# Layer 0's modulation in quarters of the features, with five products of the first layer opened between them

## The chip, the cores and the metric

The kernel runs on one core of a Trainium2 chip. The metric is the device time of one execution in microseconds (us). Engines are named as in the profile: PE is TensorE's matmuls, PEld its weight loads, DVE is VectorE, ACT is ScalarE, POOL is GpSimd, SP is SyncE, whose queue issues all DMAs here.

## What is computed

A trunk of two layers over 256 context tokens and 256 tokens of the sequence (1024 features), then a stack of attention, a recurrent mixer and two feed-forward blocks. What the change touches is the beginning of a trunk layer:

```python
silu_c, silu_cc = silu(c), silu(c_ctx)
mod   = silu_c  @ mod_w[l] + mod_b[l]        # 1024 -> 3072, for the sequence
mod_c = silu_cc @ mod_w[l] + mod_b[l]        # the same weights, for the context
shift, scale, gate = split(mod, 3)
z  = (rmsnorm(x,  pre_g) * (1 + scale)   + shift)   @ w_in     # 1024 -> columns q, kv, kr, ..., merge
zc = (rmsnorm(xc, pre_g) * (1 + scale_c) + shift_c) @ w_in
```

The columns of `w_in` are read in blocks of 128: `q` 0 and 1, `kv` 0 and `misc` (rope and gate columns) are the latents of the first attention, `px` and `pg` belong to the pool branch, `merge` to the merging gates. Everything is float32.

## The kernel before, in words

*Products.* Each weight block of up to 128 x 1024 numbers (512 KB) is loaded into a tile `wr` (`raw`, L361) and split into a high part `wh` (ScalarE, L377) and a low part `wl` (VectorE, L379). Activations are split in the same way (`split`, L385 and L386). A product of one block with all 512 tokens is 8 blocks of the contraction times three matmuls of 512 columns, high by high, low by high and high by low (`mm3`, L395 to L397), 24 matmuls that add up in one PSUM buffer. Of PSUM's eight buffers three are `mm`, three `at`, two `aux`.

*The head.* The four token tiles are loaded, normed (L429, L1175) and transposed into `xT`, features by tokens (L1179, L1180). Meanwhile the modulation runs in `mod_cols`: 2048 columns of `mod_w` in four stages of 512 columns in the order shift 0 to 511, scale 0 to 511, shift 512 to 1023, scale 512 to 1023. A stage has four loads of 512 KB; each load is multiplied with both silu vectors in small matmuls (L466), and behind the fourth `mod_rows` copies the sums out (L470), `mod_cols` transposes them (L479), adds up four groups (L482), adds the bias (L483) and for a scale stage applies 1 + scale and the norm's gain (L486). After the second stage the features 0 to 511 of `xT` are scaled and shifted (L1188) and split into `xn`, after the fourth the other half. The sixteen loads have sixteen buffers of their own.

*Layer 0.* Only then come the weight blocks of the layer: `latents` makes q0, q1, kv and misc, each with its evacuations, and column sums for the norms (L669, L671), reciprocal roots, transposes (L445) and tables. `weaves` runs a main generator and takes steps of filling generators at a given ratio per step: beside the latents and the attention (`mla`) these are the pool branch (8 steps: px0, pg0, px1, ...) and the first merge (8 steps), beside the attention also the second layer's modulation, beside the scan (`gla`) the rest of the merge, four gate steps and eight merge steps. A level of the scan is subtractions on VectorE, an exponential, two multiplications on GpSimd (L895, L915) and small matmuls (L859).

*Order.* The framework puts the instructions of each engine and queue into an order ahead of time, from the program's order, the readiness that its own time table gives, the free buffers and priorities; `high_priority` moves work ahead, and `tc.issue_after(i)` puts the instructions of a block behind instruction `i` on `i`'s engine. On the chip each engine takes its instructions in that order.

## Time and profile before

| | |
|---|---|
| median of three runs | 1546.4 us (1542.88 to 1547.67) |
| profiled execution | 1548.55 us, its span 1546.7 us |
| TensorE busy | 1485.1 us, 96% of the span |
| VectorE / ScalarE / GpSimd busy | 62% / 49% / 16% |
| read from HBM | 227.09 MB, 147 GB/s over the span |

The profile is one execution. Matmuls are pipelined and their ends are modelled, so the durations of neighbouring matmuls overlap; what one costs in a dense stretch is the distance between starts. Idle time of an engine that is not the bottleneck costs nothing.

### The profile page before, as it was taken

What the parts mean: (1) busy time and instruction counts of PE and PEld (TensorE: products, weight loads), DVE (VectorE), ACT (ScalarE), POOL (GpSimd) and SP (SyncE); (2) the same over time, 40 slices, a digit from 0 to 9 for tenths busy, and PEclk for the clock granted to TensorE, in tenths of its full rate; (3) what the DMA queues carried; (4) which work ended last, traced back from release to release, by engine and by line L of the source; (5) the groups of instructions that cost most, each with busy time, mean ns of one, the idle gap of its engine ahead of it and who ended that gap; (6) DMA issues with size and microseconds to landing.
All of it is one profiled execution on the core that took longest, in us unless ns stands there. A gap on an engine that the chain in (4) does not pass through costs nothing.

```text
span 1546.7 us, 25517 instructions
## 1 busy us (share of the span) xinstructions
PE 1485.1 (96%) x10206; PEld 1277.8 (83%) x10206; DVE 955.3 (62%) x1530; ACT 757.8 (49%) x1267; POOL 248.5 (16%) x225
## 2 busy tenths in 40 slices
PE   6999999999999999999999989999999997899998
PEld 3766668787877789878989989879999886899986
DVE  5555545866444567766786654866665567756654
ACT  4444344463423356656565454554444458534443
POOL 0101103624200000113442020321000024100000
PEclk8999999999999999999999999999999998899999
DMA  8433322223334465326446563324566654435564
GB/s 341 126 101 131 123 91 82 65 68 95 96 109 151 135 207 160 116 76 207 158 149 193 170 224 124 123 95 157 185 187 185 214 191 148 151 116 186 180 191 134
DMA packets 65639, 229.79 MB, mean 149 GB/s; under 512 B 7280, under 2 KB 7920, under 8 KB 65392
## 3 DMA queue, kind: packets, MB, share of 16 engines
q1 hardware_dynamic: 65520, 228.16, 46.0%
q8 instruction: 80, 1.31, 0.3%
q14 instruction: 39, 0.32, 0.1%
HBM read 227.09 MB, written 1.05 MB: 147 GB/s over the span
## 4 chain that ended last, share of the span: by engine, by line
PE 81%; DVE 6%; DMA 4%; issue 3%; ACT 3%; POOL 2%; SPq 0%; POOLq 0%; DVEq 0%; ACTq 0%
PE mm L395 22%; PE mm L397 22%; PE mm L396 22%; DMA wr<-in_w_dram 3%; PE at L735 2%; DVE wl L379 2%; PE aux L768 2%; ACT wh L377 2%; PE at L755 1%; PE at L859 1%; PE mm L466 1%; POOL wl L379 1%; POOL E L915 1%; POOL qp L895 1%; PE aux L466 0%
## 5 line engine op out<-in xcount | busy, mean ns | idle before, releaser
L379 DVE TENSOR_TENSOR wl<-wr,wh 128x1024 fp32r<-128x1024 f32 x339 | 425.5, 1257 | 340.2 <-ACT wh L377 338.5
L377 ACT ACTIVATE wh<-wr 128x1024 fp32r<-128x1024 f32 x352 | 370.6, 1055 | 426.3 <-PE mm L396 149.7
L395 PE MATMUL mm<-xnah,wh 128*128 128x256 f32 (+1 forms) x1192 | 368.9, 310 | 11.5 <-DVE rt L1496 10.3
L397 PE MATMUL mm<-xnah,wl 128*128 128x256 f32 (+1 forms) x1192 | 363.2, 305 | 4.0 <-DVE wl L379 4.0
L396 PE MATMUL mm<-xnal,wh 128*128 128x256 f32 (+1 forms) x1192 | 361.7, 304 | 0.0
L395 PEld LDWEIGHTS mm<-xnah,wh 128*128 128x128 f32 x1192 | 226.9, 190 | 27.4 <-DVE rt L1496 10.5
L397 PEld LDWEIGHTS mm<-xnah,wl 128*128 128x128 f32 x1192 | 226.8, 190 | 17.3 <-DVE wl L379 5.4
L396 PEld LDWEIGHTS mm<-xnal,wh 128*128 128x128 f32 x1192 | 227.1, 191 | 9.7 <-issue 1.4
L419 POOL TENSOR_TENSOR sm<-sm,minus_half 128x1 f32<-128x1 f32 (+3 forms) x34 | 26.3, 776 | 695.3 <-DVE sm L567 357.6
L397 PE MATMUL mm<-xnbh,wl 128*128 128x512 f32 (+1 forms) x392 | 136.7, 349 | 0.0
L395 PE MATMUL mm<-xnbh,wh 128*128 128x512 f32 (+1 forms) x392 | 135.0, 345 | 0.0
L396 PE MATMUL mm<-xnbl,wh 128*128 128x512 f32 (+1 forms) x392 | 134.8, 344 | 0.0
L395 PE MATMUL mm<-wh,xnah 128*128 128x256 f32 x288 | 83.4, 291 | 6.4 <-ACT xnah L385 6.1
L397 PEld LDWEIGHTS mm<-xnbh,wl 128*128 128x128 f32 x392 | 73.9, 188 | 11.8 <-issue 3.1
L395 PEld LDWEIGHTS mm<-xnbh,wh 128*128 128x128 f32 x392 | 74.0, 189 | 11.2 <-issue 2.9
L397 PE MATMUL mm<-wh,xnal 128*128 128x256 f32 x288 | 82.2, 289 | 0.8 <-DVE xnal L386 0.6
L396 PE MATMUL mm<-wl,xnah 128*128 128x256 f32 x288 | 82.7, 289 | 0.0
L396 PEld LDWEIGHTS mm<-xnbl,wh 128*128 128x128 f32 x392 | 73.9, 188 | 10.1 <-issue 1.2
L396 PE MATMUL mm<-wl,hh 128*128 128x512 f32 x176 | 69.1, 393 | 0.2 <-DVE wl L379 0.2
L397 PE MATMUL mm<-wh,hl 128*128 128x512 f32 x176 | 68.8, 391 | 0.0
L395 PE MATMUL mm<-yh,wh 128*128 128x512 f32 (+1 forms) x192 | 64.9, 338 | 0.0
L396 PE MATMUL mm<-yl,wh 128*128 128x512 f32 (+1 forms) x192 | 64.9, 338 | 0.0
(373 smaller groups left out, 2821.3 us busy)
## 6 DMA issues: line engine op xcount, KB each, us to landing
wr<-in_w_dram SPq DMA_DIRECT2D x398, 512.0 KB, 3.6
wr<-in_w_dram SPq DMA_DIRECT2D x18, 256.0 KB, 3.2
row<-in_rows_dram SPq DMA_DIRECT2D x8, 512.0 KB, 4.9
xt<-in_xin_dram SPq DMA_DIRECT2D x4, 512.0 KB, 5.7
scr<-in_rows_dram SPq DMA_DIRECT2D x8, 256.0 KB, 4.6
xr<-in_xin_dram SPq DMA_DIRECT2D x2, 512.0 KB, 4.6
xc<-in_xin_dram SPq DMA_DIRECT2D x2, 512.0 KB, 5.3
toep<-in_toep_dram SPq DMA_DIRECT2D x1, 1024.0 KB, 7.2
```

The lines of the kernel that those rows point to most:

```text
L377: S.activation(ch.h, r, AF.Copy)
L379: eng.tensor_tensor(ch.l, r, ch.h.bitcast(F32), op=OP.subtract)
L395: T.matmul(dst, lh, rh, start=first and i == 0, stop=False)
L396: T.matmul(dst, lh, rl, start=False, stop=False)
L397: T.matmul(dst, ll, rh, start=False, stop=last and i == n - 1)
L419: G.tensor_tensor(y, m, minus_half[:, :n], op=OP.pow)
L466: T.matmul(p[32 * j:32 * j + 32, c0:c0 + 256], sc[:, k * 32:k * 32 + 32], r[:, j, :], start=half == 0, stop=half == 1, tile_position=(0, 3 ...
L735: T.matmul(pa[:, :n], qxs[pr, j][:, c0 + qt * P:c0 + qt * P + P], kxs[pr, j][:, :n], start=True, stop=True)
L755: T.transpose(pa[:, k * 256 + qt * P:k * 256 + qt * P + P], r[qt][:, (2 * k2 + k) * P:(2 * k2 + k + 1) * P], ident)
L768: T.matmul(py[64 * j:64 * j + 64, c0:c0 + 256], v[:, k, h * 64:h * 64 + 64], pTs[j][k // 2][:, k % 2, :], start=k == 0, stop=k == nk - 1, ...
L859: T.matmul(pa[c * s:c * s + s, t * 2 * s:(t + 1) * 2 * s], k_[:, i:i + s], q_[:, :, j:j + s], start=True, stop=True, tile_position=(0, c * s))
L895: (V, G)[j].tensor_tensor(b[r, j, :], gq[r], e[r], op=OP.mult)
```

## The change

The modulation of both trunk layers goes through four quarters of 256 features: a quarter's four loads are two for its shift and two for its scale, so that each quarter ends with finished columns for its own features (`md.shift`, `md.scale`), at the price of one more small bias operation. In layer 0's head the rows of a quarter (two blocks of the contraction) are scaled and split right behind its columns. Between the quarters the weights of five blocks of `w_in` are loaded and split (`begin`), and the matmuls of the blocks whose rows are there are issued into PSUM buffers that stay open (`go`), in a written order. Two groups of them are put behind the last modulation matmul of a quarter on TensorE. Loads of the head share twelve buffers. The modulation's sums use `aux` buffers; three open sums use `mm`, two use `at`. `latents` and the pool branch take the finished sums from `M.ready`. The loads of layer 0's latents are put behind the head's last load on SP's queue, and the filling beside the latents runs at 0.8 a step in layer 0, where it was 0.3.

```diff
--- before.py
+++ after.py
@@ -267,6 +267,11 @@
 
 
 
+EARLY = [("q", 0), ("q", 1), ("kv", 0), ("misc", 0), ("px", 0)]
+MODBUFS = 12
+
+
+
 HEADS = '''k0 k1 z0 k2 z1 k3 z2 q0 z3 L0 q1 m0 q2 m1 s0 A0 q3 m2 A1 s1 B0 w0 m3 A2 C0 B1 s2 w1 A3 C1 B2 s3 w2 C2 B3 w3 C3'''.split()
 
 
@@ -353,20 +358,22 @@
     nlo = [0]
     ahead = [0]
     lopool = [0]
+    begun = [None, None]
 
     def raw(key, pl=wp, bufs=3, width=CW):
         t = pl.tile([P, width], F32, tag="wr", name=nm("wr"), bufs=bufs)
         _, kts, cols = SPECS[key]
         n = len(kts) * len(cols)
-        nc.sync.dma_start(t[:, :n], w[INDEX[key]][:, :n])
+        with tc.issue_after(begun[0]) if begun[0] is not None else nullcontext():
+            begun[1] = nc.sync.dma_start(t[:, :n], w[INDEX[key]][:, :n])
         return t[:, :n].rearrange("p (k c) -> p k c", k=len(kts))
 
     def W(key, pl=wp, bufs=3):
         with tc.high_priority(offset=ahead[0]):
             return W_(key, pl, bufs)
 
-    def W_(key, pl, bufs):
-        r = raw(key)
+    def W_(key, pl, bufs, *where):
+        r = raw(key, *where)
         _, nkt, n = r.shape
         ch = Obj()
         th = pl.tile([P, CW], F32R, tag="wh", name=nm("wh"), bufs=bufs)
@@ -455,43 +462,47 @@
 
     sc = const.tile([P, 256], F32, name="sc")
 
-    def mod_rows(l, cb2, ptile, *where):
+    def mod_rows(l, cbs, ptile, *where):
+
         p = ptile()
-        for cb in (2 * cb2, 2 * cb2 + 1):
-            c0 = (cb % 2) * 256
+        for n, cb in enumerate(cbs):
+            c0 = n * 256
             for half in range(2):
                 r = raw(("mod", l, cb, half), *where)
                 for j in range(4):
                     k = 4 * half + j
-                    T.matmul(p[32 * j:32 * j + 32, c0:c0 + 256], sc[:, k * 32:k * 32 + 32], r[:, j, :],
-                             start=half == 0, stop=half == 1, tile_position=(0, 32 * j))
+                    m = T.matmul(p[32 * j:32 * j + 32, c0:c0 + 256], sc[:, k * 32:k * 32 + 32], r[:, j, :],
+                                 start=half == 0, stop=half == 1, tile_position=(0, 32 * j))
                 yield
         mr = scratch()
         V.tensor_copy(mr, p)
-        return mr
-
-    def mod_cols(l, md, *where):
-        md.col = const.tile([P, 16, 2], F32, name=f"mcol{l}")
-        for cb2 in (0, 2, 1, 3):
-            mr = yield from mod_rows(l, cb2, mmps, *where)
+        return mr, m
+
+    def mod_cols(l, md, ptile, *where):
+
+        col = const.tile([P, 4, 2, 2, 2], F32, name=f"mcol{l}")
+        md.shift = lambda kk, m: col[:, kk // 2, 0, kk % 2, m:m + 1]
+        md.scale = lambda kk, m: col[:, kk // 2, 1, kk % 2, m:m + 1]
+        for q in range(4):
+            mr, md.last = yield from mod_rows(l, (q, 4 + q), ptile, *where)
             pc = auxps()
             for j in range(4):
                 T.transpose(pc[:, j * P:(j + 1) * P], mr[:, j * P:(j + 1) * P], ident)
-            cl = md.col[:, 4 * cb2:4 * cb2 + 4, :]
-            bias = VC(("shift_b", l), 4 * cb2, 4) if cb2 < 2 else VC(("scale_b", l), 4 * cb2 - 8, 4)
+            cl = col[:, q].rearrange("p a k r -> p (a k) r")
             V.tensor_reduce(cl, pc.rearrange("p (j g r) -> p j r g", j=4, g=4)[:, :, 0:2, :], axis=AX.X, op=OP.add)
-            V.tensor_tensor(cl, cl, bias[:, :, None].to_broadcast([P, 4, 2]), op=OP.add)
-            if cb2 >= 2:
-                pre = VC(("pre", l), 4 * cb2 - 8, 4)
-                V.scalar_tensor_tensor(cl, cl, 1.0, pre[:, :, None].to_broadcast([P, 4, 2]), op0=OP.add, op1=OP.mult)
-        yield
+            for i, name in enumerate(("shift_b", "scale_b")):
+                bias = VC((name, l), 2 * q, 2)
+                V.tensor_tensor(col[:, q, i], col[:, q, i], bias[:, :, None].to_broadcast([P, 2, 2]), op=OP.add)
+            pre = VC(("pre", l), 2 * q, 2)
+            V.scalar_tensor_tensor(col[:, q, 1], col[:, q, 1], 1.0, pre[:, :, None].to_broadcast([P, 2, 2]), op0=OP.add, op1=OP.mult)
+            yield
 
     def mod_gates(l, md, pl, *where):
         sels = [("selx", "gx")] + ([("selc", "gc")] if l == 0 else [])
         for _, g in sels:
             setattr(md, g, pl.tile([P, D], F32, name=nm(g)))
         for c in range(2):
-            mr = yield from mod_rows(l, 4 + c, auxps, *where)
+            mr, _ = yield from mod_rows(l, (8 + 2 * c, 9 + 2 * c), auxps, *where)
             bB, pB = rowhalf(("mod_b", l), c), rowhalf(("post", l), c)
             for sel, g in sels:
                 dst = getattr(md, g)[:, c * 512:c * 512 + 512]
@@ -534,7 +545,7 @@
             for k in range(2):
                 kk = 2 * k2 + k
                 sl = slice(k * 256, k * 256 + 256)
-                scale, shift = md.col[:, 8 + kk, m:m + 1], md.col[:, kk, m:m + 1]
+                scale, shift = md.scale(kk, m), md.shift(kk, m)
                 if k == 0:
                     S.activation(xm[:, sl], p[:, sl], AF.Identity, scale=scale, bias=shift)
                 else:
@@ -638,6 +649,8 @@
         NT = TW // P
 
         def win(name, i, t0=T0, t1=512):
+            if (name, i) in M.ready:
+                return M.ready.pop((name, i))[:, :t1 - t0]
             return ws(W(("win", l, name, i)), xn, t0, t1)
 
 
@@ -1125,7 +1138,8 @@
             mp = mkpool(st, f"mla{l}")
             pb, m1 = M.poolb(mp), M.merge(1, lambda: M.yp, True)
             fill = chain(lambda: pb, lambda: m1)
-            weaves(M.latents(mp), (fill, 0.3))
+            weaves(M.latents(mp), (fill, (0.8, 0.3)[l]))
+            begun[0] = None
             weaves(M.mla(mp), (fill, (0.45, 0.7)[l]), (modfill, 0.7))
             drain(pb)
             drain(modfill)
@@ -1151,6 +1165,7 @@
 
 
     md0, md1, M0, M1 = Obj(), Obj(), Obj(), Obj()
+    M0.ready, M1.ready = {}, {}
     right = ctx.enter_context(ExitStack())
     xnp = mkpool(right, "xnp", side="right")
     xn = halves(xnp)
@@ -1178,16 +1193,55 @@
                 for k in range(4):
                     T.transpose(p[:, k * P:(k + 1) * P], b[:, (4 * k4 + k) * P:(4 * k4 + k + 1) * P], ident)
                 S.activation(xT[:, 4 * k4:4 * k4 + 4, t * P:t * P + P], p.rearrange("p (k t) -> p k t", k=4), AF.Copy)
-        mc = mod_cols(0, md0, bd, 16)
-        for half in range(2):
-            for _ in range(9 if half == 0 else 8):
+
+        ep = mkpool(st, "early")
+        mc = mod_cols(0, md0, auxps, bd, MODBUFS)
+        accs = {}
+
+        def begin(*keys):
+            for key in keys:
+                n = len(accs)
+                ch = W_(("win", 0, *key), *((wp, 3) if n < 2 else (ep, 3)), bd, MODBUFS)
+                accs[key] = (ch, (mmps if n < 3 else atps)())
+
+        def quarter(q):
+            for _ in range(5):
                 next(mc, None)
-            for k in range(4 * half, 4 * half + 4):
+
+        def rows_of(q):
+            for k in (2 * q, 2 * q + 1):
                 for g in range(2):
                     gs = slice(g * 256, g * 256 + 256)
-                    V.tensor_scalar(xT[:, k, gs], xT[:, k, gs], md0.col[:, 8 + k, 1 - g:2 - g], md0.col[:, k, 1 - g:2 - g],
-                                    op0=OP.mult, op1=OP.add)
+                    V.tensor_scalar(xT[:, k, gs], xT[:, k, gs], md0.scale(k, 1 - g), md0.shift(k, 1 - g), op0=OP.mult, op1=OP.add)
                 split(xn, (ALL, k), xT[:, k, :])
+
+        def go(keys, k0, k1):
+            for key in keys:
+                ch, d = accs[key]
+                mm3(d, [(ch.h[:, k, :], ch.l[:, k, :], xn.h[:, k, :], xn.l[:, k, :]) for k in range(k0, k1)], k0 == 0, k1 == NK)
+
+        a, b, c, d, e = EARLY
+        quarter(0)
+        begin(a, b)
+        rows_of(0)
+        go((a, b), 0, 2)
+        quarter(1)
+        begin(c, d)
+        rows_of(1)
+        go((a, b), 2, 4)
+        go((c,), 0, 4)
+        quarter(2)
+        begin(e)
+        with tc.issue_after(md0.last.ins):
+            go((d,), 0, 4)
+        rows_of(2)
+        go((a, b, c, d), 4, 6)
+        quarter(3)
+        with tc.issue_after(md0.last.ins):
+            go((e,), 0, 6)
+        rows_of(3)
+        go(EARLY, 6, 8)
+        M0.ready.update({key: d for key, (_, d) in accs.items()})
 
 
     lam = VC("lam")
@@ -1212,7 +1266,8 @@
     V.tensor_scalar(hb[:, 8:16], VC("bi"), 0.5, None, op0=OP.mult)
     M0.lp = mkpool(left, "l0")
     trunk_layer(0, md0, xn, M0)
-    trunk_core(0, M0, mod_cols(1, md1))
+    begun[0] = begun[1].ins
+    trunk_core(0, M0, mod_cols(1, md1, mmps))
     rx = ExitStack()
     with ExitStack() as st:
         bd = mkpool(st, "bd")
```

## Rows read from the trace of the kernel before

**Rows 1.** The page: busy time by engine, and the chain that ended last.
```profile
PE 1485.1 (96%) x10206; PEld 1277.8 (83%) x10206; DVE 955.3 (62%) x1530; ACT 757.8 (49%) x1267; POOL 248.5 (16%) x225
...
PE 81%; DVE 6%; DMA 4%; issue 3%; ACT 3%; POOL 2%; SPq 0%; POOLq 0%; DVEq 0%; ACTq 0%
```

**Rows 2.** Slices of the head: stretch, length, busy time by engine, clock, DMA, GB/s.
```profile
20.00:22.00 2.00, 0.94 (x16) 0.31 (x16) 1.04 (x4) 0.00 (x0) 0.00 (x0) 1.00 1.02 406
24.00:26.00 2.00, 0.64 (x8) 0.16 (x8) 2.00 (x8) 1.60 (x3) 0.00 (x0) 0.99 1.03 404
26.00:28.00 2.00, 1.26 (x12) 0.41 (x16) 1.87 (x4) 0.91 (x2) 0.00 (x0) 0.50 1.01 406
...
34.00:36.00 2.00, 0.92 (x6) 0.48 (x4) 1.48 (x4) 1.72 (x2) 0.00 (x0) 1.00 0.04 14
36.00:38.00 2.00, 1.93 (x5) 1.55 (x6) 1.96 (x6) 1.03 (x2) 0.00 (x0) 0.55 0.38 66
38.00:40.00 2.00, 2.00 (x7) 1.57 (x6) 2.00 (x7) 1.29 (x3) 0.00 (x0) 0.59 0.76 250
```

**Rows 3.** TensorE in order of time, head: start, duration, line, operation, idle before.
```profile
15.95 1.26 PE L466 MATMUL mm<-wr,sc 128*32 128x256 f32 x16
...
20.42 0.64 PE L466 MATMUL mm<-wr,sc 128*32 128x256 f32 x8 [0.64 <-DMA wr<-in_w_dram]
...
22.27 0.66 PE L479 MATMUL aux<-ct,scr 128*128 128x128 f32 x4
22.98 0.64 PE L466 MATMUL mm<-wr,sc 128*32 128x256 f32 x8
...
26.45 1.08 PE L466 MATMUL mm<-wr,sc 128*32 128x256 f32 x8 [0.64 <-DMA wr<-in_w_dram]
...
34.20 0.48 PE L395 MATMUL mm<-xnah,wh 128*128 128x512 f32 x1
...
36.07 0.69 PE L397 MATMUL mm<-xnah,wl 128*128 128x512 f32 x1 [1.15 <-DVE wl L379]
...
39.81 0.39 PE L397 MATMUL mm<-xnah,wl 128*128 128x512 f32 x1
...
40.98 0.39 PE L397 MATMUL mm<-xnah,wl 128*128 128x512 f32 x1
...
53.86 0.40 PE L397 MATMUL mm<-xnbh,wl 128*128 128x512 f32 x1
```

**Rows 4.** TensorE's weight loads that waited for the fifth and the sixteenth modulation load.
```profile
16.57 0.16 PEld L466 LDWEIGHTS mm<-wr,sc 128*32 128x32 f32 x8 [0.47 <-DMA wr<-in_w_dram]
...
31.57 0.15 PEld L466 LDWEIGHTS mm<-wr,sc 128*32 128x32 f32 x4 [0.30 <-DMA wr<-in_w_dram]
```

**Rows 5.** VectorE and ScalarE in order of time, head.
```profile
23.59 2.68 DVE L1188 TENSOR_SCALAR xT<-xT,mcol 128x256 f32<-128x256 f32 x8
24.36 2.57 ACT L385 ACTIVATE xnah<-xT 128x512 fp32r<-128x512 f32 x4 [7.65 <-DVE xT L1188]
...
32.83 1.06 ACT L377 ACTIVATE wh<-wr 128x1024 fp32r<-128x1024 f32 x1 [5.90 <-DMA wr<-in_w_dram]
...
34.80 1.22 DVE L379 TENSOR_TENSOR wl<-wr,wh 128x1024 fp32r<-128x1024 f32 x1
...
35.93 0.16 DVE L486 SCALAR_TENSOR_TENSOR mcol<-mcol,vt 128x8 f32<-128x8 f32 x1
```

**Rows 6.** TensorE in order of time, where the five products end.
```profile
68.65 0.39 PE L397 MATMUL mm<-xnbh,wl 128*128 128x512 f32 x1
...
76.03 1.07 PE L466 MATMUL mm<-wr,sc 128*32 128x256 f32 x16
77.04 1.13 PE L735 MATMUL at<-kx,qx 128*128 128x256 f32 x4
```

**Rows 7.** Layer 0's scan: a slice of 50 us, and TensorE's long wait in it.
```profile
250.00:300.00 50.00, 48.14 (x449) 39.83 (x449) 30.84 (x46) 19.05 (x26) 23.73 (x18) 1.00 0.26 79
...
283.19 0.65 PE L859 MATMUL at<-qp,E 128*32 128x64 f32 x32 [1.69 <-POOL E L915]
```

More of the change, by code (lines that the diff above doesn't have):

```diff
@@ L1 @@
-from contextlib import ExitStack
+from contextlib import ExitStack, nullcontext
 import numpy as np
```

## The prediction

> **What bounds the kernel now.** I read the summary by engine and the chain that ended last first [rows 1]. TensorE is busy in 96% of the span and holds 81% of the chain, VectorE 6%, the DMAs 4%. So a gain has to be TensorE time: either the engine idles less or its matmuls run at the faster clock. Next I read the head in slices of two microseconds [rows 2], because the change works there. Until about 32 us the DMA engines are full (share 1.01 to 1.03, 404 to 406 GB/s) while TensorE is busy for 0.94 of 2 us in one slice and 0.64 in another; from 36 us the relation turns round. The head waits for modulation weights, everything behind it for TensorE. In the same slices the granted clock falls from 1.00 to 0.50 (26 us on), is back at 1.00 at 34, and is 0.55 at 36 to 38: the lower of the two levels (1.2 GHz) comes behind slices in which TensorE did little, the higher (2.4 GHz) behind two or three slices of dense work. Last I read TensorE's own list and the weight loads that waited for DMAs [rows 3, 4]: loads of modulation weights are taken up as they land, 1.28 us apart (20.42 to 22.98 is two of them), the sixteenth and last is taken up at 31.57, the first product begins at 34.20, waits, and TensorE is dense from 36.07.
>
> **The stretch that is compared.** Both kernels run the same 120 matmuls for the five products q0, q1, kv, misc and px0 (8 blocks of the contraction x 3 terms x 5). A matmul of 512 columns starts every 0.234 us at the full clock (40.98 to 53.86, 56 rows: 12.88 / 55) [rows 3]. Before the change two of them ran at 34.20; from 36.07 the other 118 need 27.6 us, plus 1.63 us because the nine starts from 36.07 to 39.81 took 3.74 us instead of 2.11. So the five are done 65.3 us into the span, column sums and small transposes not counted. The last such row is at 68.65 [rows 6], and the 3.6 us between are those sums and transposes, which stay in both kernels.
>
> **The change part by part.**
> *The DMAs.* Five weight blocks of 512 KB now stand among the sixteen modulation loads and no longer behind them. At 1.28 us each the last modulation load moves from 31.57 to 38.0. All of them still come as fast as the DMA engines can bring them: nine of the 21 loads need one of the twelve buffers for a second time, and the tightest (the seventeenth) needs the buffer of the fifth, which lands near 17 [rows 4] and is split soon after, some ten microseconds before its turn. I take nothing for that; a stall of one load would cost 1.28 us.
>
> *The chain of one quarter.* The last load's matmuls, a copy, four transposes, a sum over the groups, the small bias operations, the scaled rows and their split follow each other. Before, such a chain ran from 20.42 to the first split row at 24.99 (ACT 24.36 plus a fourth of 2.57) [rows 3, 5]: 4.6 us. A quarter needs one more small VectorE operation than a stage did (0.17 us) but half as many rows; I leave it at 4.6. The first quarter's four loads are through the PE at 15.95 to 16.6, so its first rows come at 20.5. The second quarter's last load is the tenth of the queue, which today is used near 23.0, so its rows come at 27.6. The third's is the sixteenth, 31.57, rows at 36.2. The fourth's is at 38.0, rows at 42.6.
>
> *TensorE's sum from 20.5.* Twelve modulation loads at 0.535 us (16 records in 1.07 us [rows 6]) make 6.4 us, three times four transposes at 0.66 us [rows 3] make 2.0, 120 matmuls make 28.1. Dense and at full clock the five products would be done at 20.5 + 36.5 = 57.0.
> What is missing from that: between 20.5 and 27.6 there are only 12 open matmuls (2.8 us), four loads (2.1) and four transposes (0.7), 5.6 us of work in 7.1 us, so 1.5 us idle. From 27.6 to 36.2 there are 36 matmuls, four loads and four transposes: 11.2 us of work for 8.6 us, covered. From there TensorE reaches 40.4, and the fourth quarter has 24 + 18 matmuls, loads and transposes beside it, 12.6 us, up to 53.0 us, while its rows come at 42.6: covered with 10 us to spare. The 30 matmuls that close the sums take the last 7.0 us. I also add 1.6 us of slow clock, as in the rows of before, since TensorE is as loosely filled between 16 and 27 as it was between 20 and 28. Forecast: 57.0 + 1.5 + 1.6 = 60.1, against 65.3, a gain of 5.2 us. The ends: 57.0 if neither loss comes (gain 8.3), and 57.0 + 1.6 + 3 x 4.6 = 72.4 if none of the later three chains is covered (loss 7.1). I choose near the good end because the work is there to cover the last two chains, by 2.6 and 10 us.
>
> *VectorE and ScalarE.* From 16.6 VectorE has 16 scalings at 0.335 (2.68 / 8 [rows 5]), 8 splits at some 0.65, 5 weight splits at 1.22, 4 copies at 0.69, 3.3 us of small operations and 4.4 us of other constants: about 27 us, done by 44, while its last rows are wanted near 53. ScalarE has less (5 x 1.06 and 8 x 0.64). Cost nothing in sum; in the order of VectorE's queue a weight split between two steps of a chain costs its 1.22 us, as it did at 34.80, behind which the bias operation came at 35.93 [rows 5]. That is bounded by five such, 6.1 us, and the 2.6 and 10 us of cover take it.
>
> *PSUM.* The five open sums hold all three product buffers and two of the three of the attention. The next product can start when q0 is evacuated; q0 is closed 24 matmuls (5.6 us) before px0, and its evacuation is under 2 us. Nothing.
>
> *The first layer's latents.* They take the finished sums; the loads behind them are put behind the last modulation load, 38.0, and have until 60. The DMA queue has nothing else then. The filling work goes in at 0.8 a step and not 0.3: over four steps that is three steps of pool work and not one, so pg0 and px1 (48 matmuls, 11.2 us) stand beside the sums, the reciprocal roots and the tables. Nothing, as TensorE is busy throughout that stretch now.
>
> *What the two steps leave behind.* Two steps of filling fewer are left for the later scan of layer 0, and its fill moves on: at its first eight levels it meets gate steps (24 matmuls, 5.6 us) where it met two merge steps (36 matmuls, 8.4 us). That is up to 5.6 us less to lay beside a stage paced by GpSimd and VectorE. Today TensorE is idle there for 1.86 of 50 us, 1.69 of it in one wait for GpSimd [rows 7]. Bounds: 1.9 us gained if that wait goes, 5.6 lost. I take 0, the side of the row, since the order within the engine lets later fill move up while the scan waits.
>
> *The second layer's modulation* has 20 steps and not 17, of which the weave still takes 17; three are drained behind the attention, two loads, 1.1 us of TensorE that is moved and not added. It is first wanted hundreds of microseconds later. Nothing.
>
> **Sum.** The profiled execution took 1548.55 us (span 1546.7 and 1.85 around it); less 5.2 it is 1543.35. It stands 2.15 us above the median of the three runs, 1546.4, so the forecast for a median is 1541.2 us.
>
> **The rivals.**
> *Dense from the first rows.* If kv's and misc's first blocks fill the hole at 20.5 to 27.6 and the clock stays up, the gain is 8.3: 1538.1. For it: in the slice 20 to 22 the clock stood at 1.00 with TensorE half idle [rows 2]. Against: kv's weights land near 25 and need two splits.
> *The clock stays low in the loose stretch.* The 12 matmuls of 20.5 to 27.6 at the slow spacing (0.43 us, as from 36.07 on) cost 2.3 us more, the four loads, at 1.08 a piece [rows 3] and not 0.535, 2.2 more; 1.5 of that falls into the idle time, so 3.0 above the dense sum beside the idle 1.5 and the 1.6 behind it: 63.1, a gain of 2.2, 1544.2. For it: between 24 and 26 TensorE did little, and from 26 it had lost the clock [rows 2]. Against: between 20 and 22 it was half idle and kept it.
> The Trainium skill (TensorE: Matmul & The Clock Gate, Part 1, What's actually happening) says that "the default state is throttled, and activity releases the throttle"; by that rule the sparse stretch would start at 1.2 GHz, which is this rival. The trace agrees in direction (0.50 behind 0.64 busy of 2 us), but shows 1.00 at 20 to 22 with 0.94.
> *The head's gain is given back in layer 0's scan.* If its stage keeps its length, the 5.6 us come back as TensorE idle: 1541.2 + 5.6 = 1546.8. For it: GpSimd's wait is there today. Against: it is one wait in nine levels.
> *Serial quarters (slower).* The matmuls of TensorE run in their written order. If a quarter's modulation matmuls are put behind products that wait for the previous quarter's rows or for a weight split, each of the later three chains, 4.6 us, stands uncovered: 72.4, 7.1 us later than before, 1553.5. It turns the gain into a loss from 6.7 us of uncovered chain on (65.3 - 57.0 - 1.6), one and a half chains. For it: today's 34.80 to 35.93 delay, and VectorE busy for 2.00 of 2 us in two slices [rows 2]. Against: the explicit order puts 12 and 18 matmuls behind the third and fourth quarter's last modulation matmul.
> The Trainium skill (same page, Architectural detail) calls ScalarE's and VectorE's queues strictly first in, first out; the delay in rows 5 agrees, and no run here shows how often it will happen.
> *The change does not take effect*, because the order finally written keeps the sums behind all modulation: then the five extra loads only stand earlier, 1546 to 1549.
>
> **How the numbers follow.** Forecast 0.42 (1539 to 1543.6), dense 0.18, low clock 0.10, given back 0.15, serial 0.13, no effect 0.02. A change of 0.3%, 4.6 us, is about what can be told from none. Faster than 1541.8: dense whole, three quarters of the forecast, a little of the rest, 0.52. Slower than 1551.0: most of serial, 0.12. The rest, 0.36, is the same. The range 1536 to 1550 leaves out some 0.06 below (a scan wait gone as well) and 0.1 above.
>
> **What would show it.** Right: TensorE's first product near 20 to 22 us, four interleaved sets of modulation matmuls, the last modulation load near 38, the first attention scores about 5 us earlier than 77.04, as many microseconds less at the end. Wrong: a last modulation load well past 38 (buffers), TensorE waits of 2 us or more for split rows between 28 and 50 (serial), a clock of 0.50 between 20 and 30 under matmuls (low clock), TensorE idle in layer 0's scan well above 1.9 us (given back).

## The result, and the profile after

The changed kernel takes 1564.82 us (median of four runs, 1561.9 to 1565.72), the kernel before 1545.52 in the same comparison (four runs, 1542.88 to 1547.67). The ratio is 1.0122 with an interval of 1.0101 to 1.0144: slower by 19 us, where 1541.2 was forecast and 1550 was the upper end of the range. The profiled execution took 1564.53 us, its span 1562.7.

The page of the changed kernel, busy time by engine and the chain that ended last, beside [rows 1]:

```profile
PE 1492.4 (96%) x10206; PEld 1284.1 (82%) x10206; DVE 949.3 (61%) x1542; ACT 757.2 (48%) x1267; POOL 250.8 (16%) x225
...
PE 77%; DVE 8%; ACT 4%; issue 3%; DMA 3%; POOL 3%; POOLq 0%; SPq 0%; DVEq 0%; ACTq 0%
```

The number of matmuls is the same and the busy time differs by 7.3 us. TensorE's share of the chain has gone from 81% to 77%; VectorE's has gone from 6% to 8%, ScalarE's from 3% to 4%, GpSimd's from 2% to 3%. So the 16.0 us of span are waits and clock, not more work. To find where they arise I read when the same instruction starts in both traces:

| start of (us) | before | after | later by |
|---|---|---|---|
| scores of the first attention | 77.0 | 85.2 | 8.2 |
| scan of layer 0 begins | 224.2 | 240.6 | 16.4 |
| last level of the scan's first half | 307.1 | 332.1 | 25.0 |
| state of the first half | 316.3 | 343.2 | 26.9 |
| state of the second half (its last matmul) | 409.7 | 439.9 | 30.2 |
| layer 1's first transposes | 575.9 | 589.8 | 13.9 |
| span | 1546.7 | 1562.7 | 16.0 |

Such a table misleads until moved work is taken out. Filling at 0.8 puts 51 matmuls of the pool branch (11.9 us at 0.234) ahead of the first scores, and two merge steps (2 x 36 x 0.234 = 16.8 us) ahead of the scan that stood behind it. So at the scores the kernel is not 8.2 us late but 3.7 early, and where the scan begins it is 0.4 early: 3.3 us of its lead are gone before the scan. Only the last two lines have the same work behind them in both kernels, and there the loss is 13.9 us when layer 1 begins and 16.0 at the end.

**The head** did what it should. TensorE in order of time, after the change (start, duration, line, operation, idle before):

```profile
23.05 1.22 PE L402 MATMUL mm<-xnah,wh 128*128 128x512 f32 x2 [2.14 <-ACT xnah L392]
...
31.97 1.93 PE L474 MATMUL aux<-wr,sc 128*32 128x256 f32 x32
...
41.49 1.93 PE L474 MATMUL aux<-wr,sc 128*32 128x256 f32 x32
...
60.65 0.40 PE L404 MATMUL at<-xnbh,wl 128*128 128x512 f32 x1
```

Slices of the head (stretch, length, busy time of PE, PEld, DVE, ACT and POOL, granted clock, DMA share, GB/s):

```profile
20.00:22.00 2.00, 0.64 (x8) 0.16 (x8) 2.00 (x9) 0.00 (x0) 0.00 (x0) 1.00 1.02 406
22.00:24.00 2.00, 0.95 (x2) 0.50 (x2) 1.97 (x7) 1.22 (x2) 0.00 (x0) 0.50 1.03 414
24.00:26.00 2.00, 2.00 (x11) 0.90 (x11) 1.64 (x5) 1.68 (x2) 0.00 (x0) 0.50 1.02 406
26.00:28.00 2.00, 2.00 (x7) 1.52 (x6) 1.63 (x2) 0.44 (x1) 0.00 (x0) 0.50 1.03 408
28.00:30.00 2.00, 2.00 (x14) 1.03 (x12) 0.00 (x0) 0.00 (x0) 0.00 (x0) 0.80 1.03 404
30.00:32.00 2.00, 2.00 (x16) 1.52 (x15) 0.69 (x1) 0.00 (x0) 0.00 (x0) 1.00 1.02 410
...
36.00:38.00 2.00, 2.00 (x10) 1.58 (x10) 1.24 (x2) 0.00 (x0) 0.00 (x0) 1.00 1.02 398
38.00:40.00 2.00, 2.00 (x13) 1.64 (x11) 0.23 (x2) 0.00 (x0) 0.00 (x0) 1.00 0.68 271
```

The last of the 120 matmuls starts at 60.65; before, by the forecast's count, they were done at 65.3. TensorE has no hole from 24 us to there (36.00 of 36 us busy from 24 to 60), is at the lower clock until 28 to 30, and the DMA engines are full until 38.

**Ahead of the scan** there is a new hole. Of the changed kernel, the first two rows are slices around the scan's begin, the third lies behind the wait of 3.15 us that is shown below, the last two are the two hundreds of microseconds in which most of the scan lies:

```profile
230.00:240.00 10.00, 10.00 (x69) 6.68 (x69) 0.69 (x1) 2.46 (x5) 0.12 (x1) 1.00 0.07 26
240.00:250.00 10.00, 7.43 (x33) 4.44 (x24) 5.65 (x10) 7.70 (x9) 3.20 (x7) 0.86 0.73 227
...
330.00:340.00 10.00, 9.29 (x42) 7.37 (x39) 0.00 (x0) 2.38 (x4) 1.93 (x2) 0.70 0.00 0
...
260.00:360.00 100.00, 94.56 (x686) 77.96 (x685) 55.06 (x74) 45.21 (x67) 38.86 (x23) 0.97 0.23 72
360.00:460.00 100.00, 95.37 (x706) 80.42 (x705) 57.19 (x82) 36.34 (x53) 38.19 (x24) 0.98 0.26 85
```

The same two stretches of time in the kernel before, whose scan begins 16.4 us earlier:

```profile
260.00:360.00 100.00, 98.14 (x747) 81.39 (x746) 66.89 (x89) 49.15 (x73) 38.98 (x24) 1.00 0.27 83
360.00:460.00 100.00, 98.61 (x666) 79.09 (x666) 54.49 (x75) 34.27 (x49) 26.23 (x17) 1.00 0.29 92
```

In these stretches TensorE is idle for 10.1 of 200 us where it was idle for 3.3, and the clock no longer stays at 1.00. Its waits there, after the change:

```profile
245.06 0.51 PE L402 MATMUL mm<-xnah,wh 128*128 128x512 f32 x1 [2.05 <-ACT wh L384]
...
301.97 0.65 PE L872 MATMUL at<-qp,E 128*32 128x64 f32 x32 [1.59 <-POOL E L928]
...
313.99 1.10 PE L872 MATMUL at<-qp,E 128*32 128x64 f32 x64
...
329.38 1.97 PE L872 MATMUL at<-qp,E 128*64 128x128 f32 x16 [3.15 <-POOL E L928]
332.07 3.78 PE L895 MATMUL at<-qp,E 128*128 128x256 f32 x8 [0.71 <-POOL E L928]
...
370.15 1.97 PE L452 MATMUL aux<-ct,sm 128*128 128x128 f32 x8 [3.23 <-POOL sm L426]
```

The wait of 1.59 us is the old one [rows 7]; those of 2.05, 3.15, 0.71 and 3.23 us are new. What releases TensorE is GpSimd, but GpSimd itself is waiting. GpSimd and VectorE of the changed kernel ahead of the 3.15 us:

```profile
312.15 2.23 POOL L928 TENSOR_TENSOR E<-E,gk 128x512 f32<-128x512 f32 x1
317.68 8.97 POOL L932 COPY A<-Ad 32x256 f32<-32x256 f32 x4 [3.31 <-DVE Ad L884]
...
328.07 1.26 POOL L928 TENSOR_TENSOR E<-E,gk 128x512 f32<-128x512 f32 x1
```

```profile
309.73 2.88 DVE L908 TENSOR_TENSOR qp<-gq,E 64x512 f32<-64x512 f32 x2
312.54 0.68 DVE L1033 TENSOR_TENSOR scr<-scr,ym 128x512 f32<-128x512 f32 x1
313.14 2.31 DVE L386 TENSOR_TENSOR wl<-wr,wh 128x1024 fp32r<-128x1024 f32 x1
315.38 0.67 DVE L459 SCALAR_TENSOR_TENSOR scr<-scr,mm 128x512 f32<-128x512 f32 x1
315.98 0.67 DVE L396 SCALAR_TENSOR_TENSOR yl<-scr,yh 128x512 fp32r<-128x512 f32 x1
316.58 0.68 DVE L1033 TENSOR_TENSOR scr<-scr,ym 128x512 f32<-128x512 f32 x1
317.18 0.43 DVE L884 COPY_PREDICATED Ad<-mk,at 128x256 f32<-128x256 int32 x1
317.51 0.41 DVE L922 TENSOR_TENSOR E<-sum 128x256 f32<-128x256 f32 x1
```

The scan's own step on VectorE, the masked copy into `Ad` at 317.18, stands behind a row of instructions without a gap: products and splits of gate steps (L1033, L396) and a weight split. TensorE's product for it is done by 315.1 (313.99 + 1.10, the next level's product included), so the copy waits for VectorE itself for two microseconds or more. Behind it GpSimd's four small copies take 8.97 us, singly (shortest, median and longest in ns, first and last start):

```profile
L932 POOL COPY A<-Ad x4: 395/2201/4050, 317.7 to 323.5; 32x256 f32<-32x256 f32 x4
```

In the kernel before the same steps look like this, on TensorE, VectorE and GpSimd:

```profile
293.49 0.65 PE L859 MATMUL at<-qp,E 128*32 128x64 f32 x32
...
294.21 0.45 DVE L871 COPY_PREDICATED Ad<-mk,at 128x256 f32<-128x256 int32 x1 [1.09 <-PE at L859]
...
294.88 0.62 DVE L910 TENSOR_TENSOR E<-sum 128x256 f32<-128x256 f32 x1
...
294.72 2.11 POOL L919 COPY A<-Ad 32x256 f32<-32x256 f32 x4 [0.46 <-DVE Ad L871]
```

There VectorE waited 1.09 us for TensorE's product and made the masked copy as soon as it was done, at 294.21 (293.49 + 0.65 = 294.14). From TensorE's product at 269.99 (after: 288.77) to this masked copy the scan took 24.2 us before and takes 28.4 now: 4.2 us are lost ahead of GpSimd's four copies, and these took 2.11 us before. VectorE was not idle beside them, in either kernel: before, its subtractions ran at some 0.61 us each between the copies, after, they run at 0.41 and the first copy takes 4.05. So the two engines took turns before, and now GpSimd is held off; what decides between the two is not shown. The gate steps' products with the attention's output (L1033 after, at 301.42, 312.54, 316.58 and 323.97) all stand within the first half's levels now; before, two stood at 303.28 and 307.86 and two behind them, at 336.08 and 341.36.

### The profile page after: what moved, and what is told of

The parts are those of the page before. It is cut to its first block, busy times and chain, and to the rows that moved or that the text cites. A ratio compares the mean times of both kernels' runs of the same rounds, so it can differ in the third digit from the quotient of the medians.

```text
span 1562.7 us, 25522 instructions
## 1 busy us (share of the span) xinstructions
PE 1492.4 (96%) x10206; PEld 1284.1 (82%) x10206; DVE 949.3 (61%) x1542; ACT 757.2 (48%) x1267; POOL 250.8 (16%) x225
## 4 chain that ended last, share of the span: by engine, by line
PE 77%; DVE 8%; ACT 4%; issue 3%; DMA 3%; POOL 3%; POOLq 0%; SPq 0%; DVEq 0%; ACTq 0%
PE mm L402 21%; PE mm L404 21%; PE mm L403 21%; DMA wr<-in_w_dram 3%; DVE wl L386 3%; PE at L748 2%; ACT wh L384 2%; PE aux L781 2%; PE at L768 1%; PE at L872 1%; PE aux L474 1%; POOL wl L386 1%; PE mm L474 1%; POOL sm L426 1%; POOL qp L908 1%
## 5 line engine op out<-in xcount | busy, mean ns | idle before, releaser
L404 PE MATMUL mm<-xnbh,wl 128*128 128x512 f32 (+1 forms) x384 | 133.2, 347 | 0.0
L403 PE MATMUL mm<-yl,wh 128*128 128x512 f32 (+1 forms) x192 | 65.3, 340 | 0.0
```

The source lines that it names most:

```text
L403: T.matmul(dst, lh, rl, start=False, stop=False)
L404: T.matmul(dst, ll, rh, start=False, stop=last and i == n - 1)
```

## The experiments

In e1 to e4, e7, e9 and e10 three edits of one line each are made singly or together: the filling's ratio beside the latents (0.3 or 0.8), its ratio beside layer 0's attention (0.45; 0.41, 0.37 and 0.33 leave one, two and three steps more for the scan, 0.37 as many as before), and the ratio at which the second layer's modulation is taken there (0.7 takes 17 of its now 20 steps, 0.84 takes all). e5, e6 and e8 move four small copies to another engine, and e11 makes the gate steps lighter. Each ratio is to the kernel before on the same chip; its medians there were 1545.09 (e1 to e4), 1546.16 (e5 to e8) and 1545.96 (e9 to e11). The five columns on the right are starts in the profiled execution, as in the table above.

| | time, us | ratio (interval) | first scores | scan begins | state, 1st half | state, 2nd half | layer 1 |
|---|---|---|---|---|---|---|---|
| before | 1545.52 | | 77.0 | 224.2 | 316.3 | 409.7 | 575.9 |
| after | 1564.82 | 1.0122 (1.0101 to 1.0144) | 85.2 | 240.6 | 343.2 | 439.9 | 589.8 |
| e1: latents 0.3 | 1554.61 | 1.0051 (1.0034 to 1.0067) | 80.9 | 229.8 | 323.7 | 417.1 | 583.3 |
| e2: 0.37 | 1546.42 | 1.0007 (0.9988 to 1.0025) | 84.7 | 223.2 | 316.3 | 409.7 | 575.9 |
| e3: before, latents 0.8 | 1563.57 | 1.0109 (1.0086 to 1.0132) | 91.5 | 245.2 | 344.8 | 441.4 | 591.3 |
| e4: modulation 0.84 | 1556.56 | 1.0069 (1.0047 to 1.0091) | 84.8 | 236.0 | 335.0 | 431.6 | 581.5 |
| e5: copies on ScalarE | 1557.88 | 1.0077 (1.0050 to 1.0103) | 84.6 | 239.9 | 340.4 | 434.8 | 585.4 |
| e6: before, copies on ScalarE | 1546.13 | 1.0 (0.9982 to 1.0018) | 78.1 | 225.2 | 318.1 | 410.7 | 577.6 |
| e7: 0.37 and 0.84 | 1540.14 | 0.9974 (0.9953 to 0.9996) | 84.6 | 219.5 | 310.5 | 403.9 | 570.1 |
| e8: e7, copies on ScalarE | 1541.36 | 0.9970 (0.9954 to 0.9986) | 84.8 | 219.6 | 311.7 | 404.3 | 571.2 |
| e9: 0.41 and 0.84 | 1540.41 | 0.9975 (0.9961 to 0.9989) | 85.8 | 227.8 | 318.6 | 413.1 | 571.6 |
| e10: 0.33 and 0.84 | 1543.03 | 0.9979 (0.9965 to 0.9994) | 84.9 | 213.2 | 303.2 | 399.1 | 572.4 |
| e11: e4, lighter gates | 1545.68 | 1.0000 (0.9984 to 1.0016) | 85.6 | 236.8 | 327.6 | 422.6 | 572.5 |

**e1, the filling beside the latents back at 0.3.**

```diff
-            weaves(M.latents(mp), (fill, (0.8, 0.3)[l]))
+            weaves(M.latents(mp), (fill, 0.3))
```

> The changed kernel with the filling beside layer 0's latents back at 0.3 a step (one step of pool work, not three), all else changed. Theory A (two fill steps were taken from layer 0's scan, which then idles): the scan gets its fill back, TensorE's idle time between 200 and 460 us falls from some 12.6 us to about 3, as before; the 4 us won in the head stay unless the latents lie open now. 1541 to 1550. Theory B (the second layer's modulation in 20 steps leaves three to be drained between attention and scan, and that delays the scan): as the changed kernel, 1562 to 1568. Theory C (any new order costs about that much): 1555 to 1565.

Measured: 1554.61 us, still slower than before, and above theory A's range although its scan recovers. The profiled execution took 1549.7 us, five less than the median; the difference lies behind the start of layer 1, from where it takes 964.7 us to the end (before 970.9), so the starts ahead of it can be read. Two things are mixed in it. The scan is as it was before (93.9 us to the first half's state, before 92.1), so two steps fewer ahead of it do undo the scan's loss. But the latents now lie open: nine matmuls more than before stand ahead of the first scores (2.1 us), so with the 4.4 us that the head gains (see below) they should come at 74.7, and they come at 80.9, 6.2 us late. TensorE in that stretch of e1:

```profile
40.00:70.00 30.00, 27.80 (x148) 21.61 (x148) 16.42 (x33) 11.51 (x20) 3.93 (x7) 0.91 0.27 97
```

It waits there 1.3 us for ScalarE's `kvnh` and 1.2 for its `mv`, and runs at 0.91 of the clock. So the raised ratio is needed to hold the head's gain; what it does later is another matter.

**e2, as many steps left for the scan as before, by the ratio beside the attention.**

```diff
-            weaves(M.mla(mp), (fill, (0.45, 0.7)[l]), (modfill, 0.7))
+            weaves(M.mla(mp), (fill, (0.37, 0.7)[l]), (modfill, 0.7))
```

> The changed kernel with 0.8 beside the latents kept and the filling beside layer 0's attention at 0.37 instead of 0.45, so that 3 + 9 = 12 steps are gone when the scan begins, as before the change. Theory A: the scan has its 16 steps of fill again, the latents stay covered: 1540 to 1545, idle time in 200 to 460 us about 3 us. Theory B: 1562 to 1568, as the drained steps are untouched. Theory C: 1555 to 1565.

Measured: 1546.42 us, no difference from before. This one line takes back 18 us of the 19. The starts in and behind the scan are to the microsecond those of before (316.3, 409.7, 575.9), and TensorE is idle as little as before in the scan's first stretch (98.31 us busy of 100, before 98.14):

```profile
260.00:360.00 100.00, 98.31 (x750) 81.73 (x749) 67.95 (x89) 49.56 (x73) 37.91 (x24) 1.00 0.27 83
```

But it is not faster than before, and so just above theory A's range, though its head is faster: something else has taken the head's 4.4 us.

**e3, the kernel before with nothing but the latents' 0.8.** The converse: the scan's loss without quarters and without open sums.

```diff
-            weaves(M.latents(mp), (fill, 0.3))
+            weaves(M.latents(mp), (fill, (0.8, 0.3)[l]))
```

> The kernel before with only the filling beside layer 0's latents at 0.8: two fill steps are taken from the scan, with the old head and the old modulation. Theory A: slower by what the changed kernel lost behind its head, 10 to 20 us: 1556 to 1566, TensorE idle over 10 us between 200 and 460 us. Theory B: no change, 1542 to 1550. Theory C: some microseconds either way.

Measured: 1563.57 us, ratio 1.0109. The old head with the moved filling is as slow as the changed kernel. GpSimd shows the same four copies as after the change:

```profile
319.94 8.97 POOL L919 COPY A<-Ad 32x256 f32<-32x256 f32 x4 [3.30 <-DVE Ad L871]
```

So the scan's loss belongs to the ratio, not to the modulation in quarters. Of e3's 15.4 us where layer 1 begins, 2.6 arise ahead of the first scores (91.5 less 77.0 and 11.9) and 10.7 between the scan's begin and its second half's state (196.2 us, before 185.5).

**e4, all steps of the second layer's modulation beside the attention.** The rival for the rest: the three steps that are drained ahead of the scan.

```diff
-            weaves(M.mla(mp), (fill, (0.45, 0.7)[l]), (modfill, 0.7))
+            weaves(M.mla(mp), (fill, (0.45, 0.7)[l]), (modfill, 0.84))
```

> The changed kernel with the second layer's modulation woven at 0.84 a step instead of 0.7, so that all 20 steps lie beside the attention and none is drained before the scan. Theory A: as the changed kernel, 1560 to 1568. Theory B: the loss behind the attention goes, 1541 to 1550. Theory C: 1555 to 1568.

Measured: 1556.56 us, between theories A and B, and layer 1 begins 8.3 us earlier than after the change. The scan keeps most of its loss: its first half takes 99.0 us (after the change 102.6, before 92.1), TensorE is busy for 93.31 of 100 us from 260 to 360, and the four copies take 8.97 us again. So the drained steps are a second cause beside the first, not a rival to it.

**e5 and e6, the four small copies on ScalarE instead of GpSimd,** in the changed kernel and in the one before. The rival for the scan: what is lost is the contention of VectorE and GpSimd.

```diff
-                            G.tensor_copy(A[0][c * 32:c * 32 + 32, :, :, c * 32:c * 32 + 32], dg[c * 32:c * 32 + 32])
+                            S.activation(A[0][c * 32:c * 32 + 32, :, :, c * 32:c * 32 + 32], dg[c * 32:c * 32 + 32], AF.Copy)
```

> The changed kernel with the four diagonal copies of a scan half (32x256 each) on ScalarE instead of GpSimd. Theory D (GpSimd's copies are held off by VectorE, which runs without a gap there; 8.97 us for the four instead of 2.11 in the kernel before, and the next level and TensorE wait behind them): the first half of layer 0's scan ends some 6 us earlier, 1553 to 1559. Theory E (the scan lacks fill for TensorE and nothing else, the copies only take the idle time up): same as the changed kernel, 1560 to 1567.

> The kernel before with the same four copies on ScalarE. Control: there GpSimd's copies take 0.50 us each and TensorE is idle for 1.9 us beside them, so both theories expect 1542 to 1549, no change; under D at most 2 us faster.

Measured: e6 1546.13 us (ratio 1.0, 0.9982 to 1.0018), nothing. e5's median is 1557.88, but its profiled execution, 1564.2, lies six above its other four (1557.2 to 1558.6), so the trace is that of the longest one. The excess lies behind the start of layer 1, from where it takes 977.0 us (after the change 972.9), so the starts ahead of it can be read. The first half takes 100.5 us from the scan's begin (after the change 102.6, before 92.1), so 2.1 of the 10.5 us lost are back; the second takes 94.4 (96.7, 93.4), and the wait of 3.23 us is gone. That cannot be laid to the copies, as the second half's four take 2.20 us in the changed kernel too. In the first half the waits for GpSimd are there without the copies. TensorE and GpSimd of e5, and its first hundred microseconds:

```profile
325.94 1.09 PE L872 MATMUL at<-qp,E 128*64 128x128 f32 x16 [1.93 <-POOL E L928]
331.03 3.65 PE L895 MATMUL at<-qp,E 128*128 128x256 f32 x8 [1.70 <-POOL E L928]
```

```profile
321.93 1.75 POOL L908 TENSOR_TENSOR qp<-gq,E 64x512 f32<-64x512 f32 x1 [7.90 <-ACT E L926]
```

```profile
260.00:360.00 100.00, 93.24 (x682) 76.45 (x681) 61.11 (x83) 48.87 (x74) 37.09 (x20) 0.98 0.23 72
```

GpSimd is idle for 7.90 us, for the exponential on ScalarE. That has two reasons. VectorE is late as before: from TensorE's product at 288.42 to the masked copy at 316.83 the scan takes 28.4 us, as after the change, so the 4.2 us lost ahead of the copies are not theirs. And the edit brings a delay of its own: VectorE's subtractions end at 318.58, the exponential starts at 320.74, as ScalarE's evacuations ahead of it are pushed back by the four copies (1.68 us) that now stand there. The time came out in theory D's range, but the first half ends 2.7 us earlier and not some six. So the copies are not what most of the first half's loss hangs on; how much of the part behind the masked copy is theirs is not shown.

**e7 and e8, both repairs, and the copies on ScalarE beside them.**

```diff
-            weaves(M.mla(mp), (fill, (0.45, 0.7)[l]), (modfill, 0.7))
+            weaves(M.mla(mp), (fill, (0.37, 0.7)[l]), (modfill, 0.84))
```

> The changed kernel with 12 fill steps gone before the scan (0.8 beside the latents, 0.37 beside the attention) and all 20 modulation steps of the second layer beside the attention (0.84). Theory F (the 4 us won in the head were lost again at the entry of the scan, where the drained modulation steps and a late weight left TensorE idle for 2.0 us and at the slow clock): the head's gain shows, 1539 to 1543. Theory G (the scan's own chain of VectorE and GpSimd takes any lead up): 1544 to 1549, with the scan's levels at the same times as before.

> As the one with 0.37 and 0.84, with the diagonal copies on ScalarE besides. D and F together: 1537 to 1542, at most 2 us below that one; G: 1544 to 1549.

Measured: 1540.14 us, ratio 0.9974 (0.9953 to 0.9996), the first version below the kernel before, by 0.6 to 7.3 us; e8 is 1541.36, so with the scan in order the copies make no difference. With e2, e4 and the changed kernel, e7 makes a square of the two edits, read where layer 1 begins: at 0.37, 575.9 falls to 570.1 by the modulation's ratio, 5.8 us; at 0.45, 589.8 falls to 581.5, 8.3 us. The other way, two steps more ahead of the scan cost 13.9 us (575.9 to 589.8) and 11.4 (570.1 to 581.5).

What the drained steps do is seen ahead of the scan. First e2, then e7, in slices:

```profile
210.00:220.00 10.00, 10.00 (x58) 7.13 (x62) 1.75 (x4) 3.55 (x7) 0.00 (x0) 1.00 0.01 2
220.00:230.00 10.00, 8.00 (x47) 4.40 (x38) 4.94 (x10) 5.06 (x7) 3.33 (x7) 0.90 0.72 213
```

```profile
200.00:260.00 60.00, 60.00 (x359) 46.10 (x358) 29.40 (x45) 28.90 (x43) 16.30 (x13) 1.00 0.30 91
```

For ten microseconds e2's DMA engines do nothing (share 0.01; 0.07 after the change), then they are at 0.72 while TensorE is idle for 2.0 us and loses clock; in e2 it waits 1.48 us for `wh` at 226.65 and 0.53 for `wl` at 227.91. e7 has no hole in 60 us. The reading: weight loads share three buffers, the loads of the drained steps hold them until TensorE comes to their matmuls, and the scan's first weights are loaded late. The waits of SyncE's DMA queue from 195 to 240 us (total, count, longest) agree; first e2, then e7:

```profile
SPq L368 <- PE mm L474: 29.0, 3, 15.7
```

```profile
SPq L368 <- PE mm L474: 7.7, 2, 6.3
```

L474 are the modulation's matmuls: e2's queue waits for them nearly four times as long as e7's. No run with more buffers was made. The hole does not account for all of the 5.8 us: TensorE's idle time is 2.0 of them, and behind it some eight matmuls start 0.43 us apart instead of 0.234, some 1.4 more. The rest has no place found for it.

**e9 and e10, one and three steps more left for the scan than after the change.** Does the loss grow with each step, or is there a threshold?

```diff
-            weaves(M.mla(mp), (fill, (0.45, 0.7)[l]), (modfill, 0.7))
+            weaves(M.mla(mp), (fill, (0.41, 0.7)[l]), (modfill, 0.84))    # e10: 0.33
```

> The changed kernel with the modulation at 0.84 and the filling beside layer 0's attention at 0.41: 13 fill steps gone before the scan (14 gave 1556.6, 12 gave 1540.1). Theory A, gradual (each step taken from the scan costs its part): about 1548, 1545 to 1552. Theory H (a threshold: the scan is upset only once gate steps fill its first half): near one of the two ends, 1540 to 1543 or 1554 to 1558. Theory C (chance of the order): anywhere, 1540 to 1560.

> The same with 0.33: 11 steps gone before the scan, one more merge step left to it. Theory A: no gain left to win, as TensorE is idle for 1.9 us there at most, but one more step drained behind it: 1538 to 1543. Theory C: anywhere between 1540 and 1560.

Measured: 14 steps gone before the scan (e4) 1556.56 us, 13 (e9) 1540.41, 12 (e7) 1540.14, 11 (e10) 1543.03. A threshold: the fourteenth step costs 16 us (14.5 by the ratios), the thirteenth nothing. Of the 16 us, 9.9 have arisen where layer 1 begins (581.5 and 571.6); the rest arises behind it, and its cause is open. The scan of e9:

```profile
260.00:360.00 100.00, 98.83 (x767) 82.27 (x766) 66.04 (x88) 48.81 (x72) 41.34 (x24) 1.00 0.23 72
```

In e9 three gate products stand among the first half's levels (292.55, 304.36, 308.15), the fourth behind them at 340.89; TensorE's waits for `E` in the scan are 3.4 us in all, the longest 1.7, as before the change (3.2 and 1.7).

**e11, e4 with lighter gate steps.** If VectorE's queue is the limit, taking VectorE work out of the gate steps has to give the scan back, at the same 14 steps. The edit leaves out the product with the attention's output, so it tells where the time goes and is no way to win it.

```diff
-                V.tensor_tensor(sg, sg, src()[:, i, :], op=OP.mult)
-                split(M.y, (ALL, i), sg, 0.5)
+                if l == 0 and name == "mg":
+                    S.activation(M.y.h[:, i], sg, AF.Copy, scale=0.5)
+                    S.activation(M.y.l[:, i], src()[:, i, :], AF.Copy, scale=0.5)
+                else:
+                    V.tensor_tensor(sg, sg, src()[:, i, :], op=OP.mult)
+                    split(M.y, (ALL, i), sg, 0.5)
```

> The changed kernel with the modulation at 0.84 and all 14 steps gone before the scan (1556.6), but layer 0's four gate steps beside the scan without two VectorE operations each: the product with the attention's output and the low part of the split are left out or made on ScalarE, so the result is another; TensorE's work is the same. Theory I (the scan's steps stand behind gate work in VectorE's queue): 5.4 us of VectorE work less, time falls to 1546 to 1552 and TensorE's waits for GpSimd in the first half of the scan fall below 3 us. Theory K (TensorE lacks fill there, whatever VectorE does): unchanged, 1553 to 1560.

Measured: 1545.68 us against e4's 1556.56. From the scan's begin the first half takes 90.8 us (e4 99.0, before 92.1), from there the second takes 95.0 (e4 96.6, before 93.4). e11's scan:

```profile
260.00:360.00 100.00, 97.32 (x738) 81.69 (x737) 60.55 (x81) 48.87 (x73) 40.63 (x27) 1.00 0.26 78
```

The waits of TensorE for `E` in the scan (total, count, longest), of e4 and of e11:

```profile
PE at L872 <- POOL E L928: 6.1, 4, 3.2
```

```profile
PE at L872 <- POOL E L928: 3.0, 3, 1.6
```

The wait is halved, and e11's first four copies take 2.11 us again. From TensorE's product at 281.90 to the masked copy at 306.69 the scan takes 24.8 us, where e4 takes 28.4 and the kernel before 24.2: with the lighter gate steps nearly all of the delay on VectorE is gone. TensorE's work is the same, so a mere lack of fill does not explain e4's loss. This supports VectorE's queue as the cause. It is not proof: the edit also gives ScalarE two instructions per gate step, and the order of everything else is planned anew for each kernel, so single microseconds here are not separable.

## Why the prediction was wrong, point by point

- **What bounds the kernel: right for the head, incomplete for the scan.** I took "everything behind it for TensorE" from the page's shares. In the scan's levels the chain runs through VectorE, ScalarE and GpSimd, and TensorE is kept busy only by what is laid beside it.
- **The DMAs: right.** The engines are full until 38 us and at 0.68 in 38 to 40. Up to 45 us the queue waited 0.4 us for TensorE's modulation matmuls and 0.3 for VectorE; nearly all the rest of its waits was for earlier loads.
- **The chain of a quarter: sized too short, without effect.** Scaled rows are split on ScalarE from 22.37, 33.54, 41.26 and 53.06 us, where I had rows at 20.5, 27.6, 36.2 and 42.6. VectorE is busy for 3.97 of the 4 us from 20 to 24, and TensorE takes the fourth quarter's four loads in one go at 41.49, when the DMA engines have been less than full since 38, as open products stand ahead of them in its order. None of it opened a hole behind 24 us, for the reason given: the open sums cover it.
- **TensorE's sum: right.** Last matmul at 60.65 + 0.23 = 60.9 against 60.1, a gain of 4.4 us against 5.2. The wait was 2.14 us where 1.5 idle stood, and the lower clock took 2.4 us of the dense slices (0.50, 0.50 and 0.80 from 24 to 30) where 1.6 stood, so the end lies between the forecast and the "low clock" rival's 63.1. "Serial quarters" did not come: TensorE waits nowhere for a later quarter's rows.
- **The latents: right in sign, and the cover was needed.** e1 shows what stood behind "Nothing": with 0.3 a step the latents open by some six microseconds.
- **What the two steps leave behind: this step failed.** I took 0 between -1.9 and +5.6, and where layer 1 begins it is +11.4 to +13.9 us (e7 to e4, e2 to after). The sign that I named for it, TensorE idle in layer 0's scan well above 1.9 us, is the one that came. I counted the moved fill in TensorE time, 24 matmuls against 36, and so had the most that could be lost at 5.6 us. What matters, as far as the runs show, is VectorE. A gate step has four VectorE instructions, some 3.3 us (1.22 + 0.67 + 0.68 + 0.68), where a step of the first merge has two or three by turns, 2.5 us on average by the same durations, beside 36 matmuls instead of 24; and it falls into levels whose own chain goes through VectorE. With 14 steps gone all four fall there, the masked copy is late by 4.2 us, GpSimd's copies behind it are held off by VectorE, TensorE waits, and the clock falls behind the waits (0.70 in 330 to 340 us). The "given back" rival had the right place and the wrong price: 5.6 us from TensorE's lack of work, where the loss came from a queue. That it was VectorE's queue is supported by e11 and by the masked copy's delay, not proved. [rows 7] showed a wait of the kind that came; I read its releaser, GpSimd, and not what GpSimd itself waited for.
- **The second layer's modulation: this step failed too.** "Moved and not added" was true of the 1.1 us of TensorE and false of the loads. The drained steps cost 5.8 us (e2 to e7) or 8.3 (after to e4), more than the head's whole gain. I priced when the weights are wanted, not what they hold until then.
- **The sum** of these: -4.4 for the head, +5.8 for the drained steps, +13.9 for the scan give +15.3 where layer 1 begins, measured +13.9. The 1.4 between is e7's: with both failed steps undone it begins layer 1 5.8 us before the kernel before and not 4.4, and 1.1 of that stands in its scan's first half (91.0 us, before 92.1); why is open. Of the 16.0 us of span 2 arise behind that point; their cause is open. e7's time is 1540.14 us, where the forecast for both steps at nothing was 1541.2: the head's term was right, and the nearness is partly luck, as the interval allows a gain of 0.6 to 7.3 us.

The Trainium skill (SBUF — State Buffer, SBUF: two separate sides) says that VectorE and GpSimd share one pair of ports under an exclusive lock, held for a whole instruction while the other blocks, where VectorE's instruction has two inputs in SBUF and GpSimd's reads SBUF. The trace agrees in that the two lengthen each other: VectorE's subtractions take some 0.61 us between GpSimd's copies before the change and 0.41 without them, and where they ran at 0.41 after it the first copy took 4.05. No run here shows which of the two gets its turn, and e5 speaks against the copies as the main cause in the first half.

## What to carry to other kernels

Filling work moved forward is taken from a later stage, and what that stage gets instead has to be counted on the engine that its chain runs through, here VectorE, not on the one that is to be kept busy. Read a wait's releaser back one step further, to what the releaser waited for, before pricing it. And when a change alters how many steps a generator has, look at where the remainder is drained and which buffers its loads hold meanwhile; the ratios that were right before are part of the change.

## What was not expected of the hardware

- GpSimd's copies of 32x256 numbers took 395 to 4050 ns, four of them 2.11 us before the change and 8.97 after it, with VectorE busy beside them both times. VectorE is lengthened too: the weight split beside GpSimd's multiplication took 2.31 us, where the page's mean is 1.26, and that multiplication took 2.23 us, where it took 1.26 beside an idle VectorE (at 330.75).
- In the head TensorE held the clock of 1.00 in 20 to 22 us with 0.64 of 2 us busy, had 0.50 in the next three slices, two of them dense, and was back at 1.00 at 30 us.
- One step of filling (36 matmuls, 8.4 us) more or less ahead of the scan made 16 us of difference in the whole kernel, the next one 0.3.
